# A gated block of four sequence mixers: S5's rotation back summed on VectorE, and the planner's paces set anew

## The chip, the cores and the metric

The kernel runs on one core of a Trainium2 chip. The metric is the device time of one execution in microseconds (us). Engines are named as in the profile: PE (TensorE, matmuls), PEld (its weight loads), DVE (VectorE), ACT (ScalarE), POOL (GpSimd) and SP (SyncE, which here only issues transfers). Transfers are issued from the queues of SP, ACT and POOL.

## What is computed

256 tokens of 2048 features pass a pre-norm, a wide projection, four sequence mixers of width 1024 (HGRN-2, S5, RWKV-7, Mamba-2), a gated sum of their up projections, an output projection, a norm and the residual. All is float32. The reference, cut to the sum and to the mixer that the change touches:

```python
h = rmsnorm(res, norm_pre)
(q_a, f_a, i_a, z_a, u_b, z_b, rkvwa_c, z_c, xbc_d, dt_d, z_d, gate_pre) = project_partitioned(h, w_in, IN_SPLITS)
...
for b in range(4):
    gate = sigmoid(gate_pre[..., b * D:(b + 1) * D] + gate_bias[b])
    merged += gate * (outs[b] @ w_up[b])
res = res + rmsnorm(merged @ w_out, norm_post)

# S5, per group of 16 channels with 64 complex states
bu_re, bu_im = u @ bbar_re, u @ bbar_im
s_re, s_im = scan of s[t] = exp(dl_re + i dl_im) * s[t - 1] + bu[t]
y = s_re @ c_re.T - s_im @ c_im.T + d * u
g = gelu(y)
out = g * sigmoid(g @ w_glu + b_glu)
```

## The kernel before

**The weight stream.** The large products read every weight once. The weights come in 444 chunks of 512 KB. A chunk is loaded to a tile `raw` (three buffers, issued from SP), split into two float32r parts, `hi` on ACT and `lo` = raw - hi on DVE (four buffers each, `_Stream.split`, L1584), and multiplied in three terms (`_Stream.products`, L1595). A chunk has 24 products of 256 columns, where features are the rows of the result ("fm"), or 12 of 512 columns, where tokens are ("tm"). Chunk j + 3 is split in the step in which chunk j is multiplied, so the split runs three chunks ahead.

The order of the stream: S5's inputs (chunks 0 to 15), Mamba-2's step sizes and convolved inputs (to 49), RWKV's (50 to 99), HGRN's (to 147), then the z parts, gates and up projections, S5's own product with `w_glu` (chunks 380 to 387), the last up projections and the output projection (412 to 443).

**The branches as jobs.** The mixers are Python generators that emit one stage at a time. A planner places the stages between the chunks. Every instruction helper books an estimated time on its engine's clock (`_Kern.book`, L162; `t_pe`, `t_dve`, `t_act`). After each chunk `run_jobs` (L1562) emits stages as long as the later of DVE's and ACT's clocks is at most AHEAD = 3.7 us ahead of PE's. `can` (L1536) lets a job go on when its last stage's booked end is at most SLACK = 1.0 us ahead of PE's clock. A product was booked at 0.427 ns per column if it is float32r (`mm`, L254), a DVE or ACT instruction at a fixed part and so much per element, whether it reads per-partition factors from a tile or not. So the booked paces decide beside which chunk a branch's stage stands in each engine's queue; how long it takes is up to the chip.

**POOL's queue.** During the stream all loads of the branches are issued from POOL (`ld`, L277, and `ldx`, L282, with `soft` set), among them S5's B and C, S5's tile operands, Mamba's, HGRN's and RWKV's inputs and the gate biases (`gb`). They leave in program order; one that waits for its source or its buffer holds those behind it.

**S5.** `s5_setup` (L1211) discretises the parameters and stores B (`ds5b`, twelve stores for the real part, twelve for the imaginary one, from `bh` and `bl`) and C transposed (`ds5c`: re, -im and, from a tile `cng`, -re) to DRAM. `s5_tile` (L1399) works on one of eight feature tiles in two halves (`hh`), 16 half tiles in all. For each it makes a cosine and a sine of the phase (`cs`), the products with B, rotates the inputs forward (`a`, `b`: tiles `ta`, `tb`; four products and two sums on DVE), runs four scans, and rotates back: a = cos * state and b = sin * state, each of 1024 elements. The state is a_re - b_im and a_im + b_re. These two sums were left to PE: `py` takes four terms, C_re a_re, -C_im b_re, -C_re b_im and -C_im a_im. Two of them go to the other half's rows of `py`, so that four groups of 32 columns of the array are in use at a time; DVE adds the two halves of rows to d * u in `cu`. `s5_load` (L1374) loads a tile's operands. Tiles 0 to 3 run before RWKV's chain ends or beside it, tiles 4 to 7 after it; the `w_glu` product needs the last one.

The generator before, at the rotation back:

```python
K.mul(a, b, cs[:, 0].unsqueeze(2).to_broadcast([128, 2, 2, 256]))
K.mul(b, b, cs[:, 1].unsqueeze(2).to_broadcast([128, 2, 2, 256]))
```

Of the kernel before, what the change touches and what calls it, by code (L numbers as in the profile page):

```python
# [60 lines left out]
PE_GAP = 0.0  # L61
# [5 lines left out]
# the functions that each activation table serves  # L67
# [6 lines left out]
class _Kern:  # L74
    """Pools, constants and instruction helpers shared by the weight stream and the branches."""

    def __init__(self, ctx, tc, drams):
# [20 lines left out]
        self.soft = False  # L98
        self.o = {}
# [12 lines left out]
    @staticmethod  # L112
    def live(tiles):
        """How many of the tiles are still referred to; the others are dropped from the list."""
        for i in range(len(tiles) - 1, -1, -1):
            if sys.getrefcount(tiles[i]) <= 2:
                del tiles[i]
        return len(tiles)
# [4 lines left out]
    def wait(self, n):  # L123
        """Until n more slots are free."""
# [5 lines left out]
    def wait_banks(self, n):  # L130
        """Until n more PSUM banks are free."""
# [5 lines left out]
    def fm(self, name, n=2):  # L137
        """A feature-major [128, 4 n, 256] array, in tiles of four feature tiles."""
        return [self.big([128, 4, 256], name=f"{name}{j}") for j in range(n)]
# [22 lines left out]
    def book(self, engine, cost, out, ins):  # L162
        """Book an instruction: it starts when the engine is free and its operands are there."""
# [31 lines left out]
    def act(self, out, in_, func, **kw):  # L195
# [7 lines left out]
        ins = [in_] + [x for x in (kw.get("scale"), kw.get("bias")) if hasattr(x, "tensor")]  # L203
        self.book("t_act", cost, out, ins)
# [4 lines left out]
    def _dve(self, out, ins, ns):  # L209
        """Book a vector instruction; one that reads the last one's output waits for it."""  # L210
        self.book("t_dve", 0.06 + ns * 1e-3, out, ins)
# [15 lines left out]
    def stt(self, out, in0, scalar, in1, op0, op1, **kw):  # L227
        self._dve(out, (in0, in1), self._n(out) * 1.045)
        return self.nc.vector.scalar_tensor_tensor(out=out, in0=in0, scalar=scalar, in1=in1, op0=op0, op1=op1, **kw)  # L229

    def ts(self, out, in0, s1, s2, op0, op1=None):
        self._dve(out, (in0,), self._n(out) * 0.53)
# [21 lines left out]
    def mm(self, out, lhsT, rhs, start=True, stop=True, **kw):  # L254
        n = self._n(rhs)
        if rhs.dtype == F32R:
            cost = n * 0.427e-3 if n >= 256 else n * 1.67e-3
        else:
            cost = max(n * 1.67e-3 * min(out.shape[0], 128) / 128, 0.027)
        self.book("t_pe", cost + PE_GAP * (1 if rhs.dtype == F32R else 2), out, (lhsT, rhs))  # L260
        return self.nc.tensor.matmul(out, lhsT, rhs, start=start, stop=stop, **kw)  # L261

    def tr(self, out, in_, b=0):
        """out = in_ transposed; in_ starts at partition b."""
# [12 lines left out]
    def ld(self, out, in_):  # L277
        """A transfer whose source may still be under way."""
# [3 lines left out]
    def ldx(self, out, in_):  # L282
        """A load of what has long been in DRAM."""
# [5 lines left out]
    def st(self, out, in_):  # L289
        """A store of what the scalar engine has just written."""  # L290
# [11 lines left out]
    def split(self, hi, lo, src):  # L302
        """src (float32 in SBUF) as the exact sum of two float32r parts."""
# [3 lines left out]
    def rstd(self, out, ss, n, eps):  # L307
        """out = 1 / sqrt(ss / n + eps), small tiles."""
# [5 lines left out]
def setup_consts(K):  # L314
    nc = K.nc
    d = K.d
# [22 lines left out]
    # ind[:, g, :] sums each half of the partitions into rows 2 g and 2 g + 1 of 32  # L339
# [15 lines left out]
    # lmask[s, level, t]: s and t (mod 64) are paired at that level of the binary split; level 0 is the diagonal  # L355
# [26 lines left out]
def head_sum(K, ps, i, sq):  # L382
    """Sums over each head's features of tile i, to rows 32 (i % 4) + 2 (i // 4) + half of ps."""
# [4 lines left out]
def bcast_heads(K, dst, src):  # L388
    """src DRAM [4, 4, 256] to dst (two tiles [128, 4, 256]): row (q, 2 g + e) on the 64 partitions of half e."""
# [5 lines left out]
# ---------------------------------------------------------------- RWKV-7  # L395
def rwkv_branch(K, rw):
    """rw: r, k, v (two tiles [128, 4, 256]) and wda [128, 256], after the token shift. Leaves K.o['c']."""
# [94 lines left out]
    # L1[c][e]: on the 64 key partitions of head parity e, rows (a | r) scaled by the decay;  # L492
    # on the other 64 partitions the masked products of k with them
# [37 lines left out]
    for c in range(4):  # L531
# [34 lines left out]
        # token-major copies of the scaled keys  # L566
# [261 lines left out]
def hgrn_half(K, g, load):  # L828
# [42 lines left out]
    k = f  # L871
# [1417 lines left out]
```

## Time and profile before

| | |
|---|---|
| time, median of 3 runs | 1427.38 us (1424.73 to 1429.43) |
| the profiled execution, its span | 1427.8 us |
| PE busy, matmuls | 1390.9 us, x9751 |
| DVE / ACT / POOL busy | 1038.0 / 827.1 / 162.0 us |
| moved | 288.62 MB, mean 202 GB/s |
| S5's output products, records on PE | 256, from 216.6 to 1212.4 us |

The span runs from the first to the last instruction; no other time of the profiled execution is given. "Busy" counts time with an instruction under way; the ends of matmuls are modelled. A float32 matmul leaves two records, a float32r one a single record. In a row, `pg` is the PSUM tile of the stream's products and `pb` that of a branch's; `h` is the normalised input, `o` a branch's output; `lo L216 <- ACT hi L207` says that a DVE instruction which writes `lo` at line 216 waited for ACT's `hi`. Lines are often those of a helper, so tiles tell more.

### The profile page before, as it was taken

How to read it: one execution, taken by the hardware profiler on the slowest of the kernel's cores; microseconds unless marked ns; L12 is line 12 of the kernel's file. 1: busy time of each engine (PE TensorE's matmuls, PEld its weight loads, DVE VectorE, ACT ScalarE, POOL GpSimd, SP SyncE). 2: the span in 40 equal slices, each digit the busy share in tenths (PEclk: the TensorE clock that was granted, in tenths of full speed). 3: DMA queues.
4: the chain of work that ended last, by engine and by line, in shares of the span. 5: the costliest groups of instructions: out<-in, count | busy, mean ns of one | idle time of the engine just before them, and what ended most of it. 6: DMA issues, size and time to landing. Idle time of an engine off the chain costs nothing.

```text
span 1427.8 us, 24645 instructions
## 1 busy us (share of the span) xinstructions
PE 1390.9 (97%) x9751; PEld 1223.2 (86%) x9751; DVE 1038.0 (73%) x1422; ACT 827.1 (58%) x1136; POOL 162.0 (11%) x268
## 2 busy tenths in 40 slices
PE   8999989989999999999999999999999999999997
PEld 7999989989989887888789888888789987888886
DVE  6787488778786784576787699767978788576655
ACT  5455445845456546765578765787556444544442
POOL 6232310010025320011100001000010000000000
PEclk9999999999999999999999999999999999999999
DMA  7878985487657876477876567655686856676664
GB/s 214 239 240 263 279 270 163 135 191 232 206 155 175 228 236 179 142 203 201 232 207 198 181 207 197 211 177 172 193 197 194 214 177 191 213 267 194 183 195 135
DMA packets 199040, 288.62 MB, mean 202 GB/s; under 512 B 12453, under 2 KB 116750, under 8 KB 198926
## 3 DMA queue, kind: packets, MB, share of 16 engines
q1 hardware_dynamic: 169614, 237.15, 54.2%
q0 software_dynamic: 25216, 43.05, 13.9%
q10 hardware_dynamic: 4096, 6.86, 1.4%
q8 instruction: 76, 1.25, 0.3%
q14 instruction: 38, 0.31, 0.1%
HBM read 268.33 MB, written 18.66 MB: 201 GB/s over the span
## 4 chain that ended last, share of the span: by engine, by line
PE 71%; DMA 8%; DVE 8%; issue 6%; ACT 6%; POOL 0%; SPq 0%; ACTq 0%; DVEq 0%; POOLq 0%
PE pg L261 63%; PE pb L261 6%; DMA raw<-in_w_in_dram 6%; DVE lo L216 4%; ACT hi L207 2%; PE pb L267 1%; DVE ta L216 1%; ACT L207 1%; DMA cn<-in_s_c_im_dram 1%; DMA x<-in_x_dram 1%; DVE invtmp L216 0%; ACT hT L207 0%; DVE tb L243 0%; DVE tb L216 0%; DMA ds5b<-bl 0%
## 5 line engine op out<-in xcount | busy, mean ns | idle before, releaser
L216 DVE TENSOR_TENSOR lo<-raw,hi 128x1024 fp32r<-128x1024 f32 x444 | 541.1, 1223 | 350.6 <-ACT hi L207 342.3
L207 ACT ACTIVATE hi<-raw 128x1024 fp32r<-128x1024 f32 x444 | 465.9, 1055 | 532.7 <-PE pg L261 249.1
L261 PE MATMUL pg<-h,hi 128*128 128x256 f32 x2624 | 480.8, 286 | 4.1 <-DVE ev L229 3.6
L261 PE MATMUL pg<-hi,h 128*128 128x512 f32 x1408 | 448.1, 393 | 0.1
L261 PEld LDWEIGHTS pg<-h,hi 128*128 128x128 f32 x2624 | 409.9, 192 | 10.7 <-issue 6.9
L261 PE MATMUL pg<-h,lo 128*128 128x256 f32 x1312 | 371.6, 285 | 5.0 <-DVE lo L216 4.1
L261 PEld LDWEIGHTS pg<-hi,h 128*128 128x128 f32 x1408 | 264.9, 188 | 58.5 <-issue 2.5
L261 PE MATMUL pg<-lo,h 128*128 128x512 f32 x704 | 275.5, 391 | 2.6 <-DVE lo L216 2.4
L261 PEld LDWEIGHTS pg<-h,lo 128*128 128x128 f32 x1312 | 251.0, 192 | 6.7 <-DVE lo L216 5.4
L261 PE MATMUL pg<-hi,o 128*128 128x512 f32 x512 | 164.2, 394 | 0.0
L261 PEld LDWEIGHTS pg<-lo,h 128*128 128x128 f32 x704 | 132.6, 188 | 30.5 <-DVE lo L216 4.5
L261 PEld LDWEIGHTS pg<-hi,o 128*128 128x128 f32 x512 | 96.1, 188 | 21.9 <-issue 1.6
L261 PE MATMUL pg<-lo,o 128*128 128x512 f32 x256 | 99.8, 390 | 0.0
L261 PE MATMUL pg<-hi,mhl 128*128 128x512 f32 x224 | 71.1, 391 | 0.0
L280 POOL DMA_DIRECT2D gb<-in_gate_bias_dram x16 | 8.7, 545 | 541.1 <-DVE gate L216 477.9
L207 ACT ACT_TABLE_LOAD x51 | 65.4, 1283 | 5.3 <-DVE mss L235 2.8
L261 PEld LDWEIGHTS pg<-lo,o 128*128 128x128 f32 x256 | 48.1, 188 | 9.5
L261 PEld LDWEIGHTS pg<-hi,mhl 128*128 128x128 f32 x224 | 42.1, 188 | 8.7
L261 PE MATMUL pg<-lo,mhl 128*128 128x512 f32 x112 | 43.6, 389 | 0.0
L243 DVE TENSOR_TENSOR_SCAN tb<-s5p,ta 128x256 f32<-128x256 f32 x64 | 41.7, 701 | 0.1
L261 PEld LDWEIGHTS pg<-lo,mhl 128*128 128x128 f32 x112 | 21.0, 188 | 4.2
L261 PE MATMUL pg<-ghl,hi 128*128 128x256 f32 x128 | 23.1, 283 | 0.0
(371 smaller groups left out, 1362.6 us busy)
## 6 DMA issues: line engine op xcount, KB each, us to landing
raw<-in_w_in_dram SPq DMA_DIRECT2D x340, 512.0 KB
raw<-in_w_up_dram SPq DMA_DIRECT2D x64, 512.0 KB
raw<-in_w_out_dram SPq DMA_DIRECT2D x32, 512.0 KB
us<-duhl POOLq DMA_DIRECT2D x16, 256.0 KB, 6.4
bs<-ds5b POOLq DMA_DIRECT2D x16, 256.0 KB, 7.6
gb<-in_gate_bias_dram POOLq DMA_DIRECT2D x16, 256.0 KB, 4.7
raw<-in_s_w_glu_dram SPq DMA_DIRECT2D x8, 512.0 KB
x<-in_x_dram SPq DMA_DIRECT2D x4, 512.0 KB
```

The costliest lines, as they stand in the source:

```text
L207: return self.nc.scalar.activation(out=out, in_=in_, func=func, **kw)
L216: return self.nc.vector.tensor_tensor(out=out, in0=in0, in1=in1, op=op)
L243: return self.nc.vector.tensor_tensor_scan(out=out, data0=data0, data1=data1, initial=0.0, op0=ALU.mult, op1=ALU.add)
L261: return self.nc.tensor.matmul(out, lhsT, rhs, start=start, stop=stop, **kw)
L267: return self.nc.tensor.transpose(out, in_, self.ident[b:b + p, b:b + p])
L280: return self.nc.gpsimd.dma_start(out=out, in_=in_)
```

## The change

Three things, beside comments and docstrings that are dropped:

1. The rotation back is finished on DVE: a_re - b_im and a_im + b_re in place, 512 elements a partition each. `py` then takes two terms, C_re with the real part and -C_im with the imaginary one; the second goes to the other half's rows as before.
2. C's third copy (-re) is not made, stored or loaded.
3. The planner's paces: a float32r product of 256 or more columns is booked at 0.417 ns per column and 13.3 ns; a change between products that use part of the array and others books 0.15 us; each per-partition factor from a tile books 0.09 us more on ACT and 0.065 us more on DVE.

```diff
-PE_GAP = 0.0
+POINTER_ACT = 0.09
+POINTER_DVE = 0.065
...
         ins = [in_] + [x for x in (kw.get("scale"), kw.get("bias")) if hasattr(x, "tensor")]
+        cost += POINTER_ACT * (len(ins) - 1)
         self.book("t_act", cost, out, ins)
...
-    def _dve(self, out, ins, ns):
-        self.book("t_dve", 0.06 + ns * 1e-3, out, ins)
+    def _dve(self, out, ins, ns, scalars=()):
+        ptr = sum(hasattr(x, "tensor") for x in scalars)
+        self.book("t_dve", 0.06 + ns * 1e-3 + POINTER_DVE * ptr, out, ins)
...
-            cost = n * 0.427e-3 if n >= 256 else n * 1.67e-3
+            cost = n * 0.417e-3 + 0.0133 if n >= 256 else n * 1.67e-3
         else:
             cost = max(n * 1.67e-3 * min(out.shape[0], 128) / 128, 0.027)
-        self.book("t_pe", cost + PE_GAP * (1 if rhs.dtype == F32R else 2), out, (lhsT, rhs))
+        parted = out.shape[0] < 128 or lhsT.shape[0] < 128
+        if parted != self.parted:
+            self.parted = parted
+            cost += 0.15
+        self.book("t_pe", cost, out, (lhsT, rhs))
...
-    dC = K.dram([8, 128, 3, 128], "ds5c")
+    dC = K.dram([8, 128, 2, 128], "ds5c")
...
-        if im == 0:
-            cng = K.big([128, 8, 128], name="cng")
-            yield 0
-            for i4 in range(2):
-                K.act(cng[:, 4 * i4:4 * i4 + 4, :], pps[i4], AF.Copy, scale=-1.0)
-            K.ld(dC[:, :, 2, :].rearrange("i p c -> p i c"), cng)
...
         K.mul(b, b, cs[:, 1].unsqueeze(2).to_broadcast([128, 2, 2, 256]))
         del cs
+        yield 0
+        K.sub(a[:, :, 0, :], a[:, :, 0, :], b[:, :, 1, :])
+        K.add(a[:, :, 1, :], a[:, :, 1, :], b[:, :, 0, :])
+        del b
         yield 1
         yield from K.wait_banks(1)
         py = K.bank([128, 2, 256])
-        for n, part in enumerate((((0, a, 0), (1, b, 0)), ((2, b, 1), (1, a, 1)))):
-            for p, (w, t, z) in enumerate(part):
-                for j in range(2):
-                    r = 64 * hh + 32 * j
-                    o = 64 * (hh ^ p) + 32 * j
-                    K.mm(py[o:o + 32, 0, :], wc[:, w, r:r + 32], t[:, j, z, :], start=(n == 0), stop=(n == 1))
-        del a, b, t
+        for z in range(2):
+            for j in range(2):
+                r = 64 * hh + 32 * j
+                o = 64 * (hh ^ z) + 32 * j
+                K.mm(py[o:o + 32, 0, :], wc[:, z, r:r + 32], a[:, j, z, :])
+        del a
```

What this does to the order, at three places. First PE, at the last half tile of S5; `cu` holds C, the number behind `hi` and `lo` is the chunk, that at the end of a name only tells tiles apart. Before:

```order
L261 MATMUL pg606_12342<-hi369_12386,h5_6_82 128x512
L261 MATMUL pb_610_12462<-ta_608_12357,cu_588_11901 32x256 x2
L261 MATMUL pb_610_12462<-tb_609_12358,cu_588_11901 32x256 x4
L261 MATMUL pb_610_12462<-ta_608_12357,cu_588_11901 32x256 x2
L261 MATMUL pg606_12342<-hi370_12406,h6_7_83 128x512
```

and now:

```order
L270 MATMUL pg602_12022<-lo350_11996,o02_547_10882 128x512
L270 MATMUL pg602_12022<-hi350_11995,o02_547_10882 128x512
L270 MATMUL pb_603_12073<-ta_599_11925,cu_580_11484 32x256 x4
L270 MATMUL pg602_12022<-hi351_12016,o03_548_10883 128x512
L270 MATMUL pg602_12022<-lo351_12017,o03_548_10883 128x512
```

Four matmuls stand where eight stood, and the block moved from behind chunk 369 to behind chunk 350.

Second DVE, at the same half tile, from the rotation back to the sums into `cu`. Before:

```order
L216 TENSOR_TENSOR ta_608_12357<-tb_609_12358,cs5_601_12283 128x1024
L216 TENSOR_TENSOR tb_609_12358<-tb_609_12358,cs5_601_12283 128x1024
L216 TENSOR_TENSOR lo371_12427<-raw371_12390,hi371_12426 128x1024
L216 TENSOR_TENSOR lo372_12445<-raw372_12410,hi372_12444 128x1024
L216 TENSOR_TENSOR lo373_12472<-raw373_12430,hi373_12471 128x1024
L229 SCALAR_TENSOR_TENSOR cu_588_11901<-cu_588_11901,pt_115,pb_610_12462 64x256
```

and now:

```order
L220 TENSOR_TENSOR ta_599_11925<-tb_600_11926,cs5_595_11856 128x1024
L220 TENSOR_TENSOR lo350_11996<-raw350_11960,hi350_11995 128x1024
L220 TENSOR_TENSOR tb_600_11926<-tb_600_11926,cs5_595_11856 128x1024
L220 TENSOR_TENSOR ta_599_11925<-ta_599_11925,tb_600_11926 128x2x256 x2
L220 TENSOR_TENSOR lo351_12017<-raw351_11980,hi351_12016 128x1024
...
L220 TENSOR_TENSOR lo354_12079<-raw354_12041,hi354_12078 128x1024
L233 SCALAR_TENSOR_TENSOR cu_580_11484<-cu_580_11484,pt_115,pb_603_12073 64x256
```

The two new sums stand behind the second product, and the result stands behind `lo354` instead of `lo373`.

Third POOL, at the end of S5's set-up: `ds5b` is B, `ds5c` is C, `mrow`, `hp`, `dbc` and `dacs` belong to Mamba's step sizes. Before:

```order
L280 DMA dbc_1128<-in_m_d_dram 128x16
...
L280 DMA ds5b<-bh_1083 32x8x128 x4
L280 DMA ds5b<-bl_1084 32x8x128 x4
L280 DMA dacs<-mrow_1131 16x256
L280 DMA ds5b<-bh_1258 32x8x128 x4
L280 DMA ds5b<-bl_1259 32x8x128 x4
...
L280 DMA cn_1638<-in_s_c_re_dram 128x8x64
L280 DMA ds5c<-cT_1884 128x8x128
L280 DMA ds5c<-cng_1930 128x8x128
```

and now:

```order
L289 DMA ds5b<-bh_1015 32x8x128 x4
L289 DMA ds5b<-bl_1016 32x8x128 x4
...
L289 DMA dbc_1148<-in_m_d_dram 128x16
...
L289 DMA ds5b<-bh_1154 32x8x128 x4
L289 DMA ds5b<-bl_1155 32x8x128 x4
...
L289 DMA cn_1216<-in_s_c_re_dram 128x8x64
L289 DMA dacs<-mrow_1151 16x256
L289 DMA ds5c<-cT_1743 128x8x128
```

The second batch of B's stores no longer stands behind `dacs`, which waits for Mamba's step sizes; ACT's copies `bh` for the two batches stand three chunks apart instead of ten. Later in the same queue the second tile's S5 loads moved from behind RWKV's `bc` loads to behind the second Mamba half's `dk` loads, and the fourth tile's from behind RWKV's `v` to behind the blocks `TT` of its inverse.

More of the change, by code (lines that the diff above doesn't have):

```diff
@@ L98, in __init__ @@
         self.soft = False
+        self.parted = False
         self.o = {}
@@ L227, in stt @@
     def stt(self, out, in0, scalar, in1, op0, op1, **kw):
-        self._dve(out, (in0, in1), self._n(out) * 1.045)
+        self._dve(out, (in0, in1), self._n(out) * 1.045, (scalar,))
         return self.nc.vector.scalar_tensor_tensor(out=out, in0=in0, scalar=scalar, in1=in1, op0=op0, op1=op1, **kw)
     def ts(self, out, in0, s1, s2, op0, op1=None):
-        self._dve(out, (in0,), self._n(out) * 0.53)
+        self._dve(out, (in0,), self._n(out) * 0.53, (s1, s2))
         if op1 is None:
@@ L1383, in s5_load @@
     ld = K.ldx if i else K.ld
-    ld(cu[:, 0:2].rearrange("p a b -> p (a b)")[:, 0:384].rearrange("p (n c) -> p n c", c=128), K.s5["C"][i])
+    ld(cu[:, 0].rearrange("p (n c) -> p n c", c=128), K.s5["C"][i])
     K.ldx(cu[:, 2], du[:, i, :])
@@ L1410, in s5_tile @@
     us, bs, cu = S.pop(i)
-    wc = cu[:, 0:2].rearrange("p a b -> p (a b)")[:, 0:384].rearrange("p (n c) -> p n c", c=128)
+    wc = cu[:, 0].rearrange("p (n c) -> p n c", c=128)
     u, g = cu[:, 2], cu[:, 3]
```

## The prediction

> **What bounds the kernel now.** I read the page's engine shares first, then the busy time by stretches, then what the TensorE (PE) waited for, then the places of those waits in the timelines of ScalarE (ACT), VectorE (DVE) and GpSimd (POOL).
>
> ```profile
> span 1427.8 us, 24645 instructions
> PE 1390.9 (97%) x9751; PEld 1223.2 (86%) x9751; DVE 1038.0 (73%) x1422; ACT 827.1 (58%) x1136; POOL 162.0 (11%) x268
> ...
> 0.00:150.00 150.00, 139.90 (x1145) 136.79 (x1146) 110.54 (x240) 83.81 (x123) 51.66 (x113) 1.00 0.81 240
> 150.00:330.00 180.00, 170.07 (x1479) 164.37 (x1478) 136.62 (x222) 97.28 (x135) 19.73 (x31) 0.97 0.77 207
> 330.00:480.00 150.00, 146.98 (x1228) 139.25 (x1227) 106.70 (x153) 88.51 (x133) 38.29 (x38) 0.99 0.70 193
> 480.00:730.00 250.00, 244.56 (x1861) 198.71 (x1860) 172.67 (x230) 147.71 (x217) 27.42 (x43) 0.99 0.73 205
> 730.00:1215.00 485.00, 484.89 (x3042) 411.23 (x3041) 386.18 (x448) 313.79 (x412) 20.68 (x35) 1.00 0.66 192
> 1215.00:1428.00 213.00, 204.47 (x1008) 172.90 (x1006) 125.26 (x134) 96.00 (x117) 4.24 (x8) 0.99 0.62 197
> ```
>
> The columns of a stretch are its length, then busy time of PE, weight loads, DVE, ACT, POOL, the granted clock, the DMA share and GB/s. PE is busy in 97%, and its idle time by stretch is 10.1, 9.9, 3.0, 5.4, 0.1 and 8.5 us. From 730 to 1215 us it never stops, though DVE works 80% of that stretch. A busy PE need not run at full pace, so I look at products in a row:
>
> ```profile
> 195.69 2.87 PE pg L261 x24
> ...
> 1035.93 2.75 PE pg L261 x12
> ```
>
> A chunk of 24 products of 256 columns takes 2.87 us (0.120 each), one of 12 products of 512 columns 2.75 (0.229 each). Both are the pace of every undisturbed chunk, so PE work is the bound, and what is taken from it comes off the time unless a wait takes its place. The waits:
>
> ```profile
> PE pg L261 <- DVE lo L216: 6.5, 8, 2.2
> PE pb L267 <- DMA npt<-in_norm_pre_dram: 4.0, 1, 4.0
> PE pg L261 <- DVE ev L229: 3.6, 1, 3.6
> PE pb L261 <- DVE cu L216: 2.7, 1, 2.7
> PE pb L261 <- DVE tb L216: 2.6, 2, 2.4
> PE pb L261 <- DVE diag L234: 2.5, 1, 2.5
> PE pb L267 <- DVE cx L235: 2.1, 1, 2.1
> PE pb L261 <- ACT xst L207: 1.3, 1, 1.3
> ...
> PE pg L261 <- DVE evm L1833: 0.8, 1, 0.8
> ...
> PE pb L261 <- DVE ta L216: 0.4, 1, 0.4
> ```
>
> (total us, times, longest.) With four smaller ones they come to 28.2 us. npt and diag (6.5) belong to the start, which keeps its order; 21.7 us depend on the order that this change rewrites.
>
> **The S5 products.** One of the 16 half tiles in the timeline of PE:
>
> ```profile
> 1101.65 0.28 PE L261 MATMUL pg<-h,lo 128*128 128x256 f32 x1
> 1101.86 0.41 PE L261 MATMUL pb<-ta,cu 128*32 128x256 f32 x2
> ...
> 1102.10 0.39 PE L261 MATMUL pb<-ta,cu 128*32 128x256 f32 x2
> ...
> 1102.32 0.39 PE L261 MATMUL pb<-ta,cu 128*32 128x256 f32 x2
> 1102.53 0.39 PE L261 MATMUL pb<-tb,cu 128*32 128x256 f32 x2
> ...
> 1102.86 0.50 PE L261 MATMUL pg<-h,hi 128*128 128x256 f32 x2
> ```
>
> Sixteen records stand for eight matmuls; four at a time start together, and the rounds begin at 1101.86, 1102.10, 1102.32 and 1102.53. The change keeps four matmuls in four different column groups, that is two rounds. What goes is 1102.53 - 1102.10 = 0.43 us; the way into the block (0.21 from the product before) and out of it (0.32) stays. 16 x 0.43 = **6.9 us less PE work**, all of it where PE is the bound. The durations of 0.39 are longer than the distance of the rounds, since ends are modelled; I go by starts. The Trainium skill (TensorE: Matmul & The Clock Gate, Measured speedup vs the span model) gives a packed group the duration of one matmul plus about 4 ns for each further tile. With 0.39 us that would be 0.40 a round and 12.8 us for the 32 rounds that go, 5.9 more than I take (1412 in the end in place of 1418); the starts here are 0.22 apart, so the trace does not bear it out.
>
> **The two additions on DVE.** Instructions of exactly their form are there already (the rotation forward):
>
> ```profile
> L216 DVE TENSOR_TENSOR ta<-ta,tb 128x512 f32<-128x512 f32 x32 | 20.6, 686 | 0.3
> ```
>
> 32 more of them are 20.6 us of DVE, 1.29 a half tile, which with 1038.0 makes 1058.6 of 1418: 75%. On the path they cost nothing as long as a half tile's products may come later: the planner emits them only when it expects their operands. PE waited for S5's own factors in two of 16 blocks (the tb row, and 0.4 for ta); if both are longer by a pair, that is +2.6, and without it 0. I take 0. The end of the branch has cover too: in the new order the last half tile's result stands behind lo354 on DVE, the glu products that need it begin with chunk 380, and 26 chunks of 2.75 are 71 us.
>
> **The third copy of C.** Gone are two ACT copies, one POOL issue, 0.5 MB written and 64 KB less read in each of eight tiles:
>
> ```profile
> L207 ACT ACTIVATE cng<-pb x2: 606/612/618, 145.5 to 146.0; 128x512 f32<-128x512 f32 x2
> L280 POOL DMA_DIRECT2D ds5c<-cng x1: 887/887/887, 146.9 to 146.9; - x1
> ```
>
> ACT is idle 42% of the time, so its 1.2 us are worth nothing by themselves. The store lies in a crowded stretch, so it goes into the next term.
>
> **The order.** The planner booked 24 x 0.1093 = 2.62 us for the first kind of chunk against 2.87 in the trace, and 2.62 against 2.75 for the second. With the new cost it books 2.88 and 2.72. So a chunk now seems longer, and more branch work is put beside it: by the two DVE orders, each row at its duration in the trace, some 15 to 40 us more DVE work stand ahead of the same chunk between chunks 110 and 370. The stretches before 730 us run at 69 to 76% DVE; the one after it runs at 80% with no PE wait, so density alone doesn't stall PE. What does is late weights:
>
> ```profile
> 89.40 1.06 ACT L207 ACTIVATE hi<-raw 128x1024 fp32r<-128x1024 f32 x1 [4.68 <-DMA raw<-in_w_in_dram]
> ...
> 174.95 1.06 ACT L207 ACTIVATE hi<-raw 128x1024 fp32r<-128x1024 f32 x1 [5.30 <-DMA raw<-in_w_in_dram]
> 179.41 1.06 ACT L207 ACTIVATE hi<-raw 128x1024 fp32r<-128x1024 f32 x1 [2.60 <-DMA raw<-in_w_in_dram]
> ...
> 306.78 1.06 ACT L207 ACTIVATE hi<-raw 128x1024 fp32r<-128x1024 f32 x1 [7.60 <-DMA raw<-in_w_in_dram]
> ```
>
> The ev wait (3.6) comes right behind the second and third, evm's 0.8 and lo's longest, 2.2, behind the last; the late load at 89.4 was covered by the chunks already split. Ahead of each stand POOL's own transfers:
>
> ```profile
> 83.74 2.33 POOL L280 DMA_DIRECT2D ds5b<-bh  x4 [0.48 <-ACT hi L207]
> 113.39 2.32 POOL L280 DMA_DIRECT2D ds5b<-bh  x4
> 161.41 0.89 POOL L280 DMA_DIRECT2D ds5c<-cT  x1 [12.73 <-issue]
> 295.36 2.50 POOL L280 DMA_DIRECT2D bc<-dinv  x4 [76.27 <-DMA dinv<-row]
> 297.84 0.64 POOL L280 DMA_DIRECT2D us<-duhl  x1
> ```
>
> And the waits for lo from 690 to 720 us alone:
>
> ```profile
> PE pg L261 <- DVE lo L216: 2.4, 4, 0.8
> ```
>
> What the new order does at each, with bounds from these rows:
> - ev, 3.6: S5's set-up ends five chunks earlier (its first products stand at chunk 46, before at 51), so the first tile's loads come ahead of the crowd, and the 0.5 MB store is gone: -2.5 (-3.6 to +3).
> - evm and lo behind 306 us, 3.0: the S5 loads no longer follow the bc loads: -2 (-3 to +2).
> - lo between 701 and 716 us, 2.4 of the 6.5: no S5 step stands between the layer norm's steps any more: -1 (-2.4 to +2).
> - cx 2.1, cu 2.7, tb 2.6, xst 1.3: same neighbours or chance: 0 (-5 to +5).
> - the two batches of B stores, 30 us apart above, follow each other with one batch's issue time (about 8 us) or little more between their starts: +1.5. The nearest row, 4.68 at 89.4, cost PE nothing; if a second one adds to it, up to +4.7.
> - a fuller DVE and ACT leave less reserve: +1 (0 to +6).
>
> Together -3, and 1427.8 - 6.9 - 3.0 = 1417.9. The profiled execution is given by its span alone, and that lies 0.4 over the median of the three runs (1427.38; they span 4.7 us), so the forecast is **1418**. About 0.3% (4.3 us) is what a measurement of this kernel can tell from no change.
>
> **The rivals.**
> - *More relief.* Planner paces near the truth work as they do after 730 us, and over half of the 21.7 us goes: 1427.8 - 6.9 - 12 = 1409. For it: 0.1 us idle in 485. Against: late weights come from transfers whose time the paces don't touch.
> - *The gain is spent.* New waits of 3 to 11 us, because PE stages are now released up to a planner's microsecond early where before each long chunk hid 0.25 us of reserve: 1424 to 1432, about 1427. For it: PE waited in ones and twos for DVE at 416 and 446 us. Against: the second kind of chunk had half that reserve and shows no waits.
> - *Transfers crowd the weights (slower).* POOL's transfers get denser in three places: the B stores, the second tile's loads behind the second Mamba half's, the fourth tile's among the inverse's blocks. Each at the price of the worst place of before (ev 3.6 + cx 2.1 = 5.7) and no relief elsewhere: 1427.8 - 6.9 + 17.1 = 1438.0. It decides from 6.9 + 4.3 = 11.2 us of added waits on, so two such places are not enough to be told slower. Beside it, the Trainium skill (DMA: Bandwidth & Descriptors, Issuing engines are not separate DMA queues) says that transfers of all issuing engines interleave on the same 16 DMA engines; the waits for raw above agree with that.
> - That the change doesn't remove the rounds can't be: half the matmuls are not issued.
>
> **How the numbers follow.** Forecast case (1412 to 1423) 0.50, more relief 0.20, gain spent 0.21, crowding 0.09. The first two are faster by over 0.3%: 0.70; the third is within it: 0.21; the last is slower: 0.09. For the range I leave out the lower half of the relief case (0.10) and, above, crowding with the end of the third: 1410 to 1428.
>
> **What would show it.** Right: each S5 block on PE shows two rounds and is 0.43 shorter; the DVE group ta<-ta,tb has 64 instructions of 0.69; PE's idle time without start and end is near 19 us, less around 180 and 300; the last S5 result comes some 60 us before the glu products. Wrong: blocks shortened by much more or less than 0.43; PE waits for lo after ACT waited for raw near 80 to 100 us (crowding); many short PE waits for DVE or ACT in pb products (gain spent); new idle time after 730 us.

## The result, and the profile after

The changed kernel takes 1475.08 us (median of 4 runs, 1471.06 to 1477.39), the kernel before 1427.37 (4 runs, 1424.73 to 1429.43): a ratio of 1.0336, 95% interval 1.0313 to 1.0360. It is slower by 47.7 us, where 9 us less were forecast. One later execution, of true_late, was slow at 2732.66 us and is left out. The profiled execution of after spans 1475.7 us, 47.9 more than that of before. First its engine shares, then its stretches (columns as in the prediction), cut where the same product stands as at the prediction's cuts:

```profile
span 1475.7 us, 24441 instructions
PE 1406.6 (95%) x9623; PEld 1233.0 (84%) x9623; DVE 1064.1 (72%) x1454; ACT 829.6 (56%) x1135; POOL 161.7 (11%) x267
```

```profile
0.00:164.00 164.00, 144.60 (x1152) 140.75 (x1153) 112.92 (x244) 84.57 (x124) 55.75 (x120) 0.98 0.81 228
164.00:349.00 185.00, 172.32 (x1457) 165.43 (x1455) 143.64 (x231) 99.47 (x140) 15.15 (x24) 0.96 0.70 187
349.00:510.00 161.00, 150.22 (x1223) 140.26 (x1222) 130.01 (x193) 87.00 (x131) 39.09 (x39) 0.98 0.67 183
510.00:771.00 261.00, 250.15 (x1837) 202.75 (x1836) 169.82 (x214) 154.52 (x229) 26.73 (x42) 0.97 0.70 197
771.00:1263.00 492.00, 484.89 (x2956) 410.98 (x2956) 382.58 (x445) 309.83 (x400) 20.69 (x35) 0.99 0.65 189
1263.00:1475.70 212.70, 204.43 (x1008) 172.87 (x1006) 125.14 (x133) 94.18 (x114) 4.25 (x8) 0.99 0.61 197
```

Every stretch up to 1263 us is longer than in before: by 14, 5, 11, 11 and 7 us; only the last is the same. 128 PE records are gone, as the change says, yet PE's busy time is 15.7 us higher and its granted clock lower. DVE's share is lower in three stretches and much higher in one (69, 78, 81, 65, 78 and 59%; before 74, 76, 71, 69, 80 and 59%), in part because the stretches are longer; its work in them differs by +2.4, +7.0, +23.3, -2.9, -3.6 and -0.1 us. What PE waited for (total us, times, longest):

```profile
PE pg L270 <- DVE lo L220: 14.4, 14, 3.0
PE pb L270 <- DVE ta L220: 7.8, 7, 3.3
PE pg L270 <- ACT hi L210: 6.4, 3, 3.3
PE pg L270 <- DVE ev L233: 5.3, 1, 5.3
...
PE pb L270 <- issue: 3.8, 2, 2.2
PE pb L276 <- DVE oa L220: 3.1, 1, 3.1
PE pb L270 <- DVE dk L220: 3.1, 2, 2.1
```

The weights' split (lo and hi) went from 6.5 to 20.8 us. Of that, 9.3 us (1.6 in before) follow a split for which ACT had itself stood waiting for the chunk's load; the rest is splits late in ACT's or DVE's queue. S5's factors went from 3.0 to 7.8; oa and dk were not waited for at all in before. A wait has a second price, which the stretch around the ev wait shows:

```profile
190.00:196.00 6.00, 0.80 (x7) 0.60 (x5) 5.92 (x10) 0.00 (x0) 0.00 (x0) 0.96 1.02 314
196.00:200.00 4.00, 3.93 (x22) 3.96 (x23) 1.12 (x1) 1.37 (x2) 0.00 (x0) 0.64 0.95 316
200.00:204.00 4.00, 3.62 (x32) 3.27 (x30) 3.88 (x7) 2.93 (x5) 0.00 (x0) 1.00 0.67 205
```

PE stands from 190.5 to 196.1; the 4 us behind that run at 0.64 of the clock, with 22 products where a full-speed stretch has 33. PE "busy" hides this: the slow products count as busy.

So I made a ledger from the starts of all PE instructions. A distance between two starts that is over 0.4 us longer than undisturbed (0.120 for products of 256 columns, 0.227 for 512, 0.112 for a branch's) is a wait; a stream product over a quarter too long is a slow one, and its excess is counted. The S5 column holds the distances inside the S5 blocks, without the waits. 12.7 us lie at the ends.

```
us               span    waits  slow products  S5 blocks  other branch work  product work
before           1427.8   27.9      23.0         16.8         126.8            1220.7
after            1475.7   63.2      34.7         12.4         132.0            1220.6
pe_pace_alone    1479.0   63.4      32.5         18.7         130.7            1221.1
half_pace        1460.1   49.0      29.1         18.8         129.9            1220.7
four_stalls      1455.8   45.3      31.9         16.8         128.4            1220.7
s5_in_old_order  1432.8   34.5      26.6         12.1         126.4            1220.5
rounds_only      1417.9   23.5      24.9          9.1         127.2            1220.6
```

After less before: 35.3 us of waits, 11.7 of slow products, 5.2 in the branches' products, 4.4 less in the S5 blocks, and nothing in the work itself: 47.8 of the 47.9 us. The S5 blocks give 4.4 and not 6.9 because only 9 of the 16 take the undisturbed 0.57 us; the others hold short waits or run at the lower clock.

### The profile page after: what moved, and what is told of

Its sections match the earlier page's. It is cut to its first block, busy times and chain, and to the rows that moved or that the text cites. A ratio compares the mean times of both kernels' runs of the same rounds, so it can differ in the third digit from the quotient of the medians.

```text
span 1475.7 us, 24441 instructions
## 1 busy us (share of the span) xinstructions
PE 1406.6 (95%) x9623; PEld 1233.0 (84%) x9623; DVE 1064.1 (72%) x1454; ACT 829.6 (56%) x1135; POOL 161.7 (11%) x267
## 4 chain that ended last, share of the span: by engine, by line
PE 55%; DVE 14%; DMA 12%; issue 10%; ACT 7%; POOL 2%; ACTq 0%; DVEq 0%; POOLq 0%
PE pg L270 50%; DMA raw<-in_w_in_dram 10%; DVE lo L220 6%; PE pb L270 4%; ACT hi L210 3%; PE pb L276 1%; DVE E L220 1%; ACT L210 1%; DVE tb L247 1%; DVE ta L220 1%; POOL GB L284 1%; ACT W L210 1%; DVE invtmp L220 1%; DVE tb L220 1%; DVE ev L233 1%
## 5 line engine op out<-in xcount | busy, mean ns | idle before, releaser
L270 PE MATMUL pg<-h,hi 128*128 128x256 f32 x2624 | 486.8, 288 | 11.0 <-DVE ev L233 5.3
L270 PEld LDWEIGHTS pg<-h,hi 128*128 128x128 f32 x2624 | 414.4, 194 | 18.5 <-issue 9.0
L270 PEld LDWEIGHTS pg<-lo,h 128*128 128x128 f32 x704 | 134.1, 190 | 33.5 <-DVE lo L220 6.8
L220 DVE TENSOR_TENSOR ta<-ta,tb 128x512 f32<-128x512 f32 x64 | 47.1, 778 | 0.6
```

Of the source, the lines that this page charges most:

```text
L220: return self.nc.vector.tensor_tensor(out=out, in0=in0, in1=in1, op=op)
```

## The experiments

Each ran beside the kernel before on the same chip; its median moved between 1427.8 and 1431.2 us from one measurement to the next, so the ratios are compared.

| run | median us | ratio to before, 95% | waits, profiled, us |
|---|---|---|---|
| s5_alone | 1448.54 | 1.0134 (1.0092 to 1.0176) | 47.5 |
| pe_pace_alone | 1480.84 | 1.0356 (1.0313 to 1.0399) | 63.4 |
| paces_alone | 1484.97 | 1.0384 (1.0347 to 1.0421) | 64.2 |
| s5_and_pe_pace | 1480.76 | 1.0360 (1.0321 to 1.0398) | 64.0 |
| four_stalls | 1459.01 | 1.0186 (1.0157 to 1.0215) | 45.3 |
| released_later | 1457.70 | 1.0186 (1.0157 to 1.0215) | 51.7 |
| shorter_lead | 1469.52 | 1.0268 (1.0229 to 1.0308) | 67.0 |
| s5_alone_first | 1477.34 | 1.0318 (1.0291 to 1.0345) | 69.2 |
| s5_true_512 | 1439.29 | 1.0073 (1.0046 to 1.0101) | 33.5 |
| s5_true_256 | 1467.58 | 1.0271 (1.0246 to 1.0297) | 58.0 |
| half_pace | 1467.08 | 1.0262 (1.0230 to 1.0293) | 49.0 |
| s5_alone_47 | 1434.98 | 1.0043 (1.0026 to 1.0060) | 33.1 |
| s5_true_late | 1435.84 | 1.0045 (1.0028 to 1.0061) | 34.2 |
| true_late | 1446.44 | 1.0126 (1.0101 to 1.0150) | 39.5 |
| before_47 | 1445.04 | 1.0109 (1.0086 to 1.0132) | 35.1 |
| s5_in_old_order | 1436.93 | 1.0055 (1.0035 to 1.0075) | 34.5 |
| rounds_only | 1422.08 | 0.9951 (0.9933 to 0.9968) | 23.5 |
| sums_only | 1432.29 | 1.0030 (1.0016 to 1.0045) | 28.3 |

### Which part of the change: the paces or S5

**s5_alone** (after, with the paces of before):

```diff
-POINTER_ACT = 0.09
-POINTER_DVE = 0.065
+POINTER_ACT = 0.0
+POINTER_DVE = 0.0
...
-            cost = n * 0.417e-3 + 0.0133 if n >= 256 else n * 1.67e-3
+            cost = n * 0.427e-3 if n >= 256 else n * 1.67e-3
...
-            cost += 0.15
+            cost += 0.0
```

> The S5 change with the planner's old paces (after with pointer costs 0, switch cost 0, 0.427 ns a column). Theory A (the true paces take away the reserve that each chunk had, so that products start before their operands are there): the order keeps the old reserve, PE's stalls stay near the 27.9 us of before, the S5 blocks give their 6.9 us back, and the only new cost is at the end of S5, whose last two half tiles stand at chunk 379, right ahead of the glu products at 380: a stall of 5 to 12 us there. 1421 to 1434 us. Theory B (the change itself is at fault: 20.6 us more DVE work on a DVE that is already the second bound): stalls as in after, 55 us and more, 1455 to 1475. Theory C (every new order costs about the same, whatever made it): 1440 to 1470, stalls at places of its own.

**pe_pace_alone** (before, one line):

```diff
-            cost = n * 0.427e-3 if n >= 256 else n * 1.67e-3
+            cost = n * 0.417e-3 + 0.0133 if n >= 256 else n * 1.67e-3
```

> The kernel before with one line changed: a product of 256 columns is booked at 0.120 us in place of 0.109, one of 512 at 0.227 in place of 0.219. S5 keeps its four terms, pointer and switch costs stay 0. Theory A: the stalls of after come without the S5 change, 1460 to 1490 us, stalls of 50 us and more. Theory B: as before, 1420 to 1440. Theory C: 1440 to 1470.

**paces_alone** (after with the S5 part undone: the two sums out, four terms and `cng` back as in before).

> All the new paces with S5's four terms and third copy of C put back. Theory A: after plus the S5 rounds, 1475 + 7 = 1482 (1470 to 1492). Theory B: 1420 to 1440. Theory C: 1440 to 1480.

**s5_and_pe_pace** (after, without the pointer costs):

```diff
-POINTER_ACT = 0.09
-POINTER_DVE = 0.065
+POINTER_ACT = 0.0
+POINTER_DVE = 0.0
```

> After without the costs of pointer operands on ACT and DVE (both 0); the products' pace, the switch cost and the S5 change stay. Theory A: the products' pace is what takes the reserve, so 1465 to 1485, about as after. If instead the pointer costs make the difference, 1420 to 1440. Theory B: 1465 to 1485 too. Theory C: 1440 to 1480.

One line, the products' booked pace, makes a loss as large as the whole: pe_pace_alone is slower than before by 3.6%, with S5 untouched and as much waiting as after (63.4 us). The pointer costs are not it. Theory B falls: with the old paces S5's new form has 28 us of waits outside one place, as before has in all. That place is S5's end, on PE:

```profile
1234.79 0.64 PE L270 MATMUL pb<-ta,cu 128*32 128x256 f32 x8
1235.36 0.74 PE L270 MATMUL pb<-us,bs 128*128 128x256 f32 x4
1255.02 1.58 PE L270 MATMUL pb<-ta,cu 128*32 128x256 f32 x8 [18.91 <-DVE ta L220]
```

The glu products come next and need this half tile, so PE stood for the chain of the last one, start to end. A planner that thinks PE faster than it is gives the branches too little room: S5 with its two sums is 18.9 us late. That is a cost of the S5 change that the true paces take away, at a far higher price elsewhere. So theory A has the place right, but its 1421 to 1434 us was missed, since the wait is 18.9 us and not 5 to 12; 1448.5 lies in theory C's range.

### Is it the pace, by its size and place

**half_pace** (before):

```diff
-            cost = n * 0.427e-3 if n >= 256 else n * 1.67e-3
+            cost = n * 0.422e-3 + 0.0067 if n >= 256 else n * 1.67e-3
```

> The kernel before with the products booked half way between the old and the true pace (0.115 us for 256 columns, 0.223 for 512), nothing else. Theory A (reserve): a time between those of before (1427) and of pe_pace_alone (1481), 1440 to 1468. Theory C (any other order costs about the same 40 to 55 us, whatever its pace): 1468 to 1482; a threshold would show as 1425 to 1435.

**s5_true_512** (s5_alone):

```diff
-            cost = n * 0.427e-3 if n >= 256 else n * 1.67e-3
+            cost = n * 0.443e-3 if n >= 512 else n * 0.427e-3 if n >= 256 else n * 1.67e-3
```

> The S5 change with the true pace for products of 512 columns alone (0.227 us booked); those of 256 columns keep 0.109, pointer and switch costs 0. Up to about 480 us the order is that of s5_alone; S5's last half tile stands at chunk 373 in place of 379. Theory A (a chunk booked short of its time leaves a reserve; it is needed in the first 480 us, where chunks of 256 columns run among crowded transfers): stalls before 480 us near the 16 us of s5_alone, the 19 us wait at the end of S5 gone, 1415 to 1432. If the reserve is needed everywhere alike: new waits from 480 us on, 1440 to 1460.

**s5_true_256** (s5_alone):

```diff
-            cost = n * 0.427e-3 if n >= 256 else n * 1.67e-3
+            cost = n * 0.427e-3 if n >= 512 else n * 0.469e-3 if n >= 256 else n * 1.67e-3
```

> The other half: the S5 change with the true pace for products of 256 columns (0.120 us booked), those of 512 keep 0.219, pointer and switch costs 0. Theory A: the waits of the first 480 us come back (30 us and more there, 16 in s5_alone and in before 19), S5 ends at chunk 367 and is not waited for: 1450 to 1480. If it is the 512 pace that costs: 1420 to 1440.

The time rises with the pace: 1, 1.026, 1.036. Half the pace makes over two thirds of the loss, though: 1467.1 us stands at the border between theory A (to 1468) and theory C (from 1468), so this run alone doesn't tell a lost reserve from an order that is worse by itself. The largest waits, of pe_pace_alone and then of half_pace:

```profile
PE pg L261 <- DVE lo L216: 17.4, 23, 3.0
PE pb L267 <- ACT cbt L207: 6.4, 1, 6.4
PE pg L261 <- ACT hi L207: 6.1, 6, 2.0
```

```profile
PE pg L261 <- DVE lo L216: 12.7, 14, 4.3
```

Waits for lo are 6.5, 12.7 and 17.4 us at the old, the half and the true pace. From the timelines I took, for chunks 10 to 439, the time from the end of a chunk's lo on DVE to the first product that reads it: it is under 2 us in 60, 82 and 95 chunks. That is the reserve going. The count doesn't measure the loss, however: it is 69 in after, which waits as long as pe_pace_alone, and 76 in sums_only (below), which waits no longer than before. S5's change with the true pace for 256 columns alone is 2.7% slower than before, as expected; with that for 512 alone it is 0.7%, where 1415 to 1432 was expected: a miss, by a 3.7 us wait for oa at 1077 us and others of 1 to 2 us. So the reserve is wanted late in the stream too, though less.

**released_later** and **shorter_lead** give reserve back to after in two other ways:

```diff
-SLACK = 1.0
+SLACK = -1.0
```

> After with SLACK = -1.0 in place of 1.0: the next stage of a branch is emitted only when the planner's TensorE is a microsecond past the time at which the stage's operands are booked, and no longer up to one before. Theory A (the true paces took the reserve between stages): the waits for branch tiles (ta, Y, xD, dk, oa, ev) mostly go; 1425 to 1450. Rival F (the reserve that was lost is that of the weights' split, which stands behind more branch work on DVE and ACT): waits for lo and hi stay, 1455 to 1475.

```diff
-AHEAD = 3.7
+AHEAD = 2.5
```

> After with AHEAD = 2.5 in place of 3.7: branch work is emitted only while VectorE and ScalarE are booked less than 2.5 us ahead of TensorE. Rival F: the splits stand behind 1.2 us less branch work, the waits for lo and hi (20.8 us in after) mostly go; 1435 to 1455. Theory A in its form by stages: the waits for branch tiles stay and those for lo and hi shrink little; 1460 to 1480.

Releasing a stage 2 us later takes 1.5 of the 3.4% back. The waits of released_later, then of shorter_lead:

```profile
PE pb L270 <- ACT Zs L210: 8.9, 1, 8.9
PE pg L270 <- DVE ev L233: 7.7, 1, 7.7
PE pg L270 <- DVE lo L220: 5.9, 7, 3.0
```

```profile
PE pg L270 <- DVE lo L220: 9.4, 10, 2.9
PE pb L270 <- DVE ta L220: 9.1, 4, 4.1
PE pg L270 <- ACT hi L210: 7.4, 5, 4.7
```

Neither theory holds for both. The later release came out at rival F's time, but with the waits for lo down from 14.4 us, which that rival expected to stay, and two long ones for branch tiles instead. The shorter lead came out as theory A says, in time and in waits: meant for lo and hi, it left 16.8 of their 20.8 us and gave back 0.7%.

### What a wait costs

**four_stalls** (before; `stall` is a cleared tile, so the result is the same):

```diff
+STALL = {246: 26, 262: 3, 288: 7, 310: 14}
...
         if u.kind == "tm":
+            if j in STALL:
+                X = K.stall
+                w, m = X[:, 0:128], X[:, 0:32]
+                K.nc.tensor.matmul(ps[:, 0, 0:32], w, m, start=False, stop=False)
+                for _ in range(STALL[j]):
+                    K.nc.gpsimd.memset(X, 0.0)
+                K.nc.tensor.matmul(ps[:, 0, 0:32], w, m, start=False, stop=False)
             self.tm(u, c, hi, lo, (0, 1))
```

> The kernel before, in its own order, with four waits of TensorE put into the stretch that had none: at chunks 246, 262, 288 and 310 a small product with zeros reads a tile, GpSimd then clears that tile 26, 3, 7 and 14 times in a row (about 0.3 us each), and a second such product waits for it. Waits of about 7.5, 1, 2 and 4 us, 14.5 together. Theory D (a wait costs more than itself: the granted clock of TensorE falls behind a wait of 2 us or more): windows of 4 to 6 us behind the waits show 0.6 to 0.8 of the clock behind the longer ones and 1.00 behind the 1 us one; the time rises by 18 to 26 us. Theory E (a wait costs its length, the lower mean clock of after is something else): the clock stays at 1.00 behind them, the time rises by 12 to 16 us.

The four waits were 9.7, 1.2, 2.7 and 5.3 us, 18.9 in all. The stretches of three of them and the 6 us behind all four (the granted clock is the third column from the end):

```profile
831.00:841.10 10.10, 0.39 (x4) 0.26 (x2) 6.01 (x8) 1.06 (x1) 8.10 (x26) 0.61 0.53 157
841.10:847.10 6.00, 6.00 (x16) 4.79 (x17) 0.00 (x0) 0.12 (x1) 0.00 (x0) 0.52 0.00 0
847.10:853.10 6.00, 6.00 (x28) 4.94 (x27) 3.96 (x5) 5.00 (x6) 0.00 (x0) 1.00 0.29 87
...
896.80:902.80 6.00, 6.00 (x54) 4.85 (x55) 5.61 (x8) 1.82 (x3) 4.10 (x7) 1.00 0.81 181
978.00:981.00 3.00, 0.30 (x5) 0.19 (x3) 3.00 (x3) 2.96 (x4) 2.28 (x8) 1.00 0.74 222
981.00:987.00 6.00, 6.00 (x28) 4.98 (x28) 1.80 (x3) 5.94 (x10) 1.44 (x3) 1.00 0.49 134
1051.00:1056.60 5.60, 0.32 (x3) 0.21 (x3) 3.66 (x6) 5.01 (x7) 4.36 (x14) 0.87 0.66 199
1056.60:1062.60 6.00, 6.00 (x27) 4.57 (x29) 0.00 (x0) 0.29 (x1) 0.00 (x0) 0.56 0.00 0
```

Theory D holds for the two longer waits: behind them PE runs at about half the clock for some 6 us. Behind 1.2 us it keeps the clock, and also behind 2.7 us, where theory D expected a loss. In the profiled executions 18.9 us of waiting cost 28.0 us, 1.48 for one; by the ratio it is 26.6 (22 to 31). Of the 9.1 us beyond the waits the two slow stretches explain 5.5 (6 us at 0.48 and at 0.44 less than full clock); most of the rest is lost behind waits that before has too, where the clock is at half for 23.9 us here and for 17.1 in before. So 1.48 is no constant. Over the twenty traces, for waits with no other within 9 us, the slow products' excess in the 9 us behind is 0.3 us on average for a wait of 1 to 1.5 us (46 of them), 0.6 for 2 to 2.5 (21), 1.5 for 3 to 3.5 (10) and 1.7 for 4 to 5 (9). The Trainium skill (TensorE: Matmul & The Clock Gate, Part 1: The HAM clock gate) says that an idle window of about 3.4 us, counted by a free-running clock, halves PE's clock until a window has been busy. The traces agree on the half, and in the clock's records it lasts 3.4 us or a multiple of it (before has five of 3.4 ahead of its end). A slow-down (an excess over 0.8 us) stands behind all 21 such waits of 3.5 us and more, and already behind 8 of the 21 of 2 to 2.5 us.

### What S5's change is worth by itself

**s5_alone_first** (s5_alone, S5 ahead of HGRN in the planner's choice):

```diff
-PRIO_S5 = 5
+PRIO_S5 = 1
```

> The S5 change with the old paces (as s5_alone), and S5's steps ahead of the other late branches in the planner's choice (PRIO_S5 = 1 in place of 5), so that its last half tile stands at chunk 371 and no longer at 379, nine chunks before the glu products. Theory A: the 19.1 us wait at the end of S5 and what follows it go, the rounds' 6.9 us stay won: 1415 to 1428. Theory B (the change is at fault by its DVE work): 1440 or more, with the waits spread. Theory C: 1440 to 1470.

The theories missed: 1477 us is in theory B's range (1440 or more), but the waits are not spread. S5's end was no longer waited for, and HGRN's last tile was instead.

```profile
PE pb L270 <- ACT hq L210: 14.6, 1, 14.6
PE pb L270 <- DVE E L220: 8.4, 8, 1.7
PE pb L276 <- DVE oa L220: 6.3, 1, 6.3
```

With the old paces there isn't room before the end for all branch work and the sums too; the priority only picks who is late.

**s5_alone_47** (s5_alone) and its control **before_47** (before), both with

```diff
-AHEAD = 3.7
+AHEAD = 4.7
```

> s5_alone with AHEAD = 4.7 in place of 3.7 (branch work up to 4.7 us ahead of the booked TensorE), which brings S5's last half tile from chunk 379 to 375 and the other branches forward too. If the wait at S5's end is only a matter of these few chunks: it shrinks from 19 to under 9 us, 1420 to 1435. If more work ahead takes the same reserve as the true pace does: new waits before 750 us, 1440 to 1470.

> The kernel before with AHEAD = 4.7: the control of s5_alone_47 (1435). If the S5 change gives its 6.9 us at equal settings: 1438 to 1444, the longer lead costs. If the S5 change gives nothing because its DVE work spends it: 1430 to 1437.

**s5_true_late** (s5_alone) and its control **true_late** (before), both with the true pace from chunk 200 on:

```diff
-            cost = n * 0.427e-3 if n >= 256 else n * 1.67e-3
+            cost = (n * 0.417e-3 + 0.0133 if self.true else n * 0.427e-3) if n >= 256 else n * 1.67e-3
...
     def products(self, j):
...
+        K.true = j >= 200
```

> The S5 change with the old paces up to chunk 200 (about 690 us) and the products' true pace from there on. Up to chunk 200 the order is that of s5_alone, whose waits there were 23.6 us (before: 27.9 in the same stretch); behind it more branch work fits beside a chunk, and S5's last half tile stands at chunk 367 in place of 379. Theory A (the reserve is needed where DVE and the weights run late, in the first 700 us, and the end needs the room): the 19 us wait goes without new ones: 1412 to 1425, faster than before. If the reserve is needed behind 700 us as well: new waits from 700 to 1150 us, 1430 to 1445. If the S5 change has no gain in itself: 1427 to 1435.

> The kernel before (four terms) with the products' true pace from chunk 200 on: the control of s5_true_late, from which the S5 change alone is told at equal paces. Up to chunk 200 the order is that of before. If the true pace costs nothing where there were no waits: 1424 to 1431, and s5_true_late lies 7 us lower (the rounds) or more. If it costs there too: 1435 to 1450.

Whether the S5 change is faster at equal settings depends on the setting. It is by 0.66 points of the ratio with the longer lead and by 0.81 with the late true pace, the intervals apart; with all new paces by 0.48 (after against paces_alone, intervals overlapping). With the products' pace (and the switch cost, which s5_and_pe_pace keeps) it gains nothing, and at the settings of before it loses 1.3 points (s5_alone). The 1412 to 1425 of theory A for s5_true_late was missed: S5's end is no longer waited for, but 8.6 us of waits stand between 700 and 1190 us, where s5_alone has 2.8. And both controls are 1.1 and 1.3% slower than before. true_late has the order of before up to chunk 200 and 19 us of waits behind 700 us, where before had 3. So the order of before is better than its neighbours in each way tried, and none of the versions with S5's new form and another setting beats it.

**s5_in_old_order**, **rounds_only** and **sums_only** hold the order of before. The first (before; its planner books as before):

```diff
         del cs
+        for z, op in enumerate((ALU.subtract, ALU.add)):
+            K.nc.vector.tensor_tensor(out=a[:, :, z, :], in0=a[:, :, z, :], in1=b[:, :, 1 - z, :], op=op)
         yield 1
...
-                    K.mm(py[o:o + 32, 0, :], wc[:, w, r:r + 32], t[:, j, z, :], start=(n == 0), stop=(n == 1))
+                    K.book("t_pe", 0.107, py[o:o + 32, 0, :], (wc[:, w, r:r + 32], t[:, j, z, :]))
+        for z in range(2):
+            for j in range(2):
+                r = 64 * hh + 32 * j
+                o = 64 * (hh ^ z) + 32 * j
+                K.nc.tensor.matmul(py[o:o + 32, 0, :], wc[:, z, r:r + 32], a[:, j, z, :], start=True, stop=True)
```

> The S5 change in the order of before, word for word: the planner books the eight products of a half tile as before and the two sums at nothing, so that the only differences are 32 sums more on VectorE and two rounds fewer in each S5 block (the third copy of C stays). If the change gives by itself what the pairs at equal settings showed (10 us: 1446.7 to 1435.8, 1445.0 to 1435.0, 1485.0 to 1475.1): 1416 to 1422. If the prediction's 6.9 us of rounds are its whole gain: 1419 to 1424. If the order of before leaves no room on VectorE for 20.6 us more: new waits at the S5 blocks and for lo, 1427 to 1440.

rounds_only is this without the two sums:

> As s5_in_old_order, without the two sums, so that the products leave out the part of the result that comes from tb. The rounds alone, in the order of before. By the starts (0.43 us a block): 1427 - 7 = 1420 to 1422. By a block of four matmuls taking one matmul's duration: 1427 - 13 = 1413 to 1416.

sums_only is before with the sums written to `cs`, ahead of `del cs`:

> The kernel before with its four terms, and 32 sums of the same form added on VectorE behind the rotation, into a tile that nobody reads any more. VectorE's 20.6 us alone, in the order of before. If they lie beside TensorE's work, as the prediction took it (0, bound +2.6): 1427 to 1431. If the order of before has no room for them: 1433 to 1450, waits for tb and lo longer by a pair of sums (1.3 to 1.6 us) each.

The rounds alone are worth 0.49% (0.32 to 0.67), 7.0 us. The sums alone, off the path, cost 0.30% (0.16 to 0.45), 4.3 us, between the two ranges that were expected; the trace has no more than 0.4 us of added waits, so where the rest lies isn't shown. Both together, with the products behind the sums, are 0.55% slower (0.35 to 0.75), 7.9 us. So in this order the sums cost 14.8 us (1.0055 less 0.9951). The waits for `ta` in s5_in_old_order, then in rounds_only:

```profile
PE pb L1476 <- DVE ta L1461: 9.9, 5, 4.4
```

```profile
PE pb L1474 <- DVE ta L216: 1.2, 2, 0.8
```

8.7 us more of waiting, now for the sums, at five places in four of the 16 blocks, are more than half of it.

## Why the prediction was wrong, step by step

- **The rounds, -6.9: right.** An undisturbed block of after on PE:

```profile
251.58 0.28 PE L270 MATMUL pg<-h,lo 128*128 128x256 f32 x1
251.79 0.64 PE L270 MATMUL pb<-ta,cu 128*32 128x256 f32 x8
252.36 0.50 PE L270 MATMUL pg<-h,hi 128*128 128x256 f32 x2
```

  From the block's first start to the next product it is 0.57 us, 1.00 before: 0.43 less. rounds_only, where all 16 blocks take 0.55 to 0.57 us, gives 7.0 us. The 12.8 us of the other sum, by one matmul's duration a round, didn't come.
- **The sums, 0 on the path (bound +2.6): failed.** "As long as a half tile's products may come later" did not hold. The prediction found two waiting blocks and priced one pair at each; the held order has four, and 14.8 us. In after the new order did move the products behind the sums, and the waits for S5's factors still grew by 4.8 us. One of them:

```profile
464.45 0.62 PE L270 MATMUL pb<-ta,cu 128*32 128x256 f32 x4 [3.27 <-DVE ta L220]
466.08 1.07 PE L270 MATMUL pb<-ta,cu 128*32 128x256 f32 x4 [1.01 <-DVE ta L220]
```

- **The order, -3: failed, and this is the step that decides.** The argument was that the planner, once it knows the true paces, works as it did after 730 us, with 80% on DVE and no waits, since "density alone doesn't stall PE". Density by stretch indeed says little: the first, the fourth and the fifth have less of it than in before and lose 32 us, with 2.4 us more, 2.9 less and 3.6 less DVE work. What changed is how late each split and each factor is. The prediction named that, as "a fuller DVE and ACT leave less reserve: +1 (0 to +6)" and as the rival "the gain is spent", 3 to 11 us; in after the waits rose by 35.3 us, and the one line with the pace costs 52 us in all (pe_pace_alone). The reason given against that rival, that chunks of 512 columns had half the reserve and no waits, also fails: the prediction's own 2.4 us for lo between 701 and 716 us are in such chunks, and s5_true_512 and true_late have more there.
- **The list of waits.** ev rose from 3.6 to 5.3, where 2.5 less were expected; cu and xst went, as chance has it, and dk, oa and Y came. The two batches of B stores, +1.5 with a bound of 4.7, now follow each other, and ACT's load of weights behind them shows it:

```profile
111.02 1.06 ACT L210 ACTIVATE hi<-raw 128x1024 fp32r<-128x1024 f32 x1 [8.69 <-DMA raw<-in_w_in_dram]
```

  PE waited 4.1 us there (3.3 for hi, 0.8 for lo): inside the bound. This is the crowding rival's first place, and 4.1 us are a small part of the 35.3. How much crowding adds elsewhere is not shown: pe_pace_alone can't tell, since there the second batch of stores starts as early (95.8 us, 94.8 in after, 113.4 in before), and of its waits for lo and hi, too, 9.2 us follow late loads. Nor is a late load a matter of transfers alone. With three buffers a load is issued when the split three chunks earlier is done (here at 99.45 us, behind a lo that ended at 99.42), so a late split makes the next load late. This one took 11.6 us from its issue to its split; the planner books 4.4 for a chunk's load (`book_dma`).
- **A wait at its length: failed.** Slow products behind the waits added 11.7 us, and the branches' products, which slow down with them, part of 5.2. The clock's records give about the same sum: leaving out the end of the span it is at half for 17.1 us in before and for 51.2 in after, and half of the difference is 17.
- **S5's end: right in after** (no wait before the glu products), and the true paces are what buys it, as s5_alone shows.

What stays open: the 52 us of the true pace may hold three things, the reserve that goes, loads that come late, and the loss of an order that happened to fit. before_47, whose order is another by a longer lead alone, costs 16 us and true_late, with the true pace behind chunk 200 alone, 18 us, but no run separates the three.

## What to carry to other kernels

A planner's error in an engine's pace can be the reserve that covers what it books short or not at all (late transfers, slow neighbours); before making an estimate true, find out which waits it covers, and put that reserve back in a place of its own. Price a wait on PE above its length from 2 us on: in these traces the clock sometimes fell behind it, and behind lone waits of 3.5 us and more it did each time. And before counting an instruction on a half-idle engine as free, look at who waits for it: off the path the 20.6 us of sums cost 4 us, in front of the products 15.

## What the runs showed of the hardware

Two-input instructions on DVE were slow here while POOL selected on a tile. S5's last factor and sums ahead of the block at 464 us on DVE, and POOL beside them:

```profile
460.46 2.17 DVE L220 TENSOR_TENSOR tb<-tb,cs 128x1024 f32<-128x1024 f32 x1
462.67 3.36 DVE L220 TENSOR_TENSOR ta<-ta,tb 128x512 f32<-128x512 f32 x2
```

```profile
459.35 2.21 POOL L284 TENSOR_SCALAR_AFFINE_SELECT GB<-GB 64x1024 f32<-64x1024 f32 x1 [8.43 <-ACT GB L210]
461.63 2.03 POOL L284 TENSOR_SCALAR_AFFINE_SELECT L<-L 64x1024 f32<-64x1024 f32 x1
...
464.31 1.18 POOL L284 TENSOR_SCALAR_AFFINE_SELECT GB<-GB 64x1024 f32<-64x1024 f32 x1
```

The pair of sums takes 3.36 us in place of 1.29, the product 2.17 in place of 1.22; POOL's selections take up to 2.21 in place of the 1.16 to 1.18 that they take where DVE stands idle. The ends look like turns: the selection of 459.35 ends at 461.56, the product behind it 1.07 us later at 462.63, the next selection 1.03 later at 463.66, each about its own undisturbed time or less behind the other's end. That one waits for the other is read from these rows; no run tests it. The Trainium skill (SBUF — State Buffer, Who interferes with whom) says that a DVE instruction with two inputs in SBUF contends with a GpSimd instruction that reads SBUF; these rows agree. Instructions of DVE that took over 1.4 times and 0.3 us more than the median of their form lost 6.1 us in before and 11.6 in after, nearly all of it between 400 and 500 us. The planner books nothing for it.
